# First layer's modulation vectors 2 and 3: four column groups side by side, in eight steps inside the spatial gate's projection

## The chip, the core and the metric

One core of one Trainium2 chip runs the kernel. The metric is the device time of one execution in microseconds (us); the time of a kernel is the median over its runs. The engines are TensorE (PE in the profile, with PEld for its weight loads), VectorE (DVE), ScalarE (ACT), GpSimd (POOL) and SyncE (SP), whose queue issues nearly all the DMAs here.

## The reference, cut to what matters

Two layers of a diffusion backbone on 512 latent and 256 context tokens of width 1024. A layer begins with a modulation: from a conditioning vector it makes six vectors of 1024 (shift, scale and gate of the two sub-layers).

```
def adaln(cvec, w, b, n):
    m = jax.nn.silu(cvec) @ w[:, : n * D_MODEL] + b[: n * D_MODEL]
    return jnp.split(m, n, axis=-1)
...
cmod = adaln(c_ctx, w_mod[l], b_mod[l], 2 if last else 6)
sh1, sc1, g1, sh2, sc2, g2 = [m[:, None, :] for m in adaln(c, w_mod[l], b_mod[l], 6)]
hl = modulate(rms_norm(x_lat, norm1_g[l]), sh1, sc1)
pa, q, k, v, pc = project(hl, P, rope)          # gate A, attention B, convolution C
x_lat = x_lat + g1 * mixer_merge(pa, o, pc, P, lam_init)
h2 = modulate(rms_norm(x_lat, norm2_g[l]), sh2, sc2)
x_lat = x_lat + g2 * conv_ffn(h2, P)
```

Vectors 0 and 1 are needed before the first projection. Vector 2 (gate of the mixing sub-layer) is needed when that sub-layer's output is added, and vector 3 (shift of the channel sub-layer) after that. This case is about vectors 2 and 3 of the first layer, for the latent and the context condition at once: a product of a 2-row matrix with 1024 x 2048 weights.

## The kernel before, in words

**Order of the work.** The program is written as one long list of operations. A scheduler puts each engine's instructions in an order ahead of time: among what is ready in its plan, it takes the earliest in the text, moved by priority offsets (`low(n)` makes a block later, `tc.high_priority` earlier). On the chip every engine goes through its own list in that order; waits are semaphores. All loads named here are issued by SP's queue, in order too.

**The stages around the change.** In layer 0 the projection of the normed tokens (`hhi`, `hlo`, split in two parts for precision) goes over column blocks in the order C (convolution branch), A (spatial gate), K, Q, V. Each block is four chunks of weights (`k2`), each loaded as `raw` (3 buffers, L215), split into `whi` (ACT, L224) and `wlo` (DVE or POOL, L110). Block C is L476 to L488. Blocks A, K, Q and V are in `proj_tok` (L425): for each chunk, six token tiles with four products each (L433, L434), then six tiles with two products each (L441). Each of these 12 tiles is a "step", 48 in all, and a list of hooks may put other work behind a given step.

Block C's result goes through a sigmoid into `cin`, and a depthwise convolution of 31 taps runs on DVE (`cacc`, L691, lowest priority) beside blocks A to Q. Block A's result goes through gelu, a layer norm (L522 to L541, ending in `vbh` and `vbl`) and four small products with the position weights (`pg`, L548), which hooks put behind steps 18 to 25 of block K; transposes (`pt`, L558) follow. The position weights are split into two slots of the `mraw` buffers (L542). The convolution's norm begins with a product `cm` (L653) behind step 41 of block Q.

**Modulation vectors 2 and 3** are made by `mod_rows` (L152), called at L502 to L510 inside `low(RLOW)` with RLOW = 250. The condition, as `cs`, is the stationary operand: 32 columns per slice of 128 inputs, 2 of them used. The weights are the moving operand, 512 columns at a time, so a product uses 32 of the 128 columns of the array. Slice k goes to column group k % 4 (`tile_position=(0, 32 * (k % 4))`), and slices 0 to 3 and 4 to 7 add up in the group's 32 partitions of one PSUM tile `mr`:

```
def part(o, k, w):
    r = 32 * (k % 4)
    T.matmul(o[r:r + 32], cs[:, k], w, start=k < 4, stop=k >= 4, tile_position=(0, r))
...
for k2 in range(KD // 2):
    raw = rp.tile([P, 2, 512], F32, tag=rtag, name="mraw", bufs=rb)
    nc.sync.dma_start(out=raw, in_=w_modH[chunks[0][0] - 2, chunks[0][1] // 4, k2])
    for a in range(2):
        part(acc.rearrange("p c q -> p (c q)"), 2 * k2 + a, raw[:, a])
```

There are four such tiles (2 vectors, 2 halves), so 16 loads of 512 KB into 4 `mraw` buffers and 32 products. Each tile is copied by ACT (`mrow`, L175); then four small products with `sel` (`mt`, L180) add up the four groups and turn the rows into columns, and one DVE addition (L185) puts in the bias.

Vectors 0 and 1 go the same way in pieces of 128 columns (L163 to L167), beside block C.

Of the kernel before, what the change touches and what calls it, by code (L numbers as in the profile page):

```python
# [9 lines left out]
F32 = mybir.dt.float32  # L10
# [6 lines left out]
P = 128  # L17
DM = 1024
KD = DM // P
# [10 lines left out]
COL_A, COL_Q, COL_K, COL_V, COL_C = 0, 512, 1024, 1536, 2048  # L30
# [11 lines left out]
NOSYNC = mybir.DependencyInfo(mybir.DependencyClass.NoSync, mybir.DependencyReason.DATA)  # L42
# [6 lines left out]
MRB, MRW, RAWB, NSQ, NTB, KXB, FTB = 4, 2, 3, 2, 3, 3, 2  # L49

HP, SCP, RSP = 1000, 2, 60
DLOW, RLOW = 150, 250
CLOW = (4000, 1000)

WE = "dpdpdpdddppdpppppddp"
# [25 lines left out]
def tile_backbone(  # L81
# [6 lines left out]
    nc = tc.nc  # L88
    V, S, G, T = nc.vector, nc.scalar, nc.gpsimd, nc.tensor
# [16 lines left out]
    def low(n):  # L106
        return tc.high_priority(offset=-n)
# [44 lines left out]
    def mod_rows(cs, sel, chunks, ps, tag, bufs, rp, rtag, rb):  # L152


        n = len(chunks)
        acc = ps.tile([P, 4, P], F32, tag=tag, name="mr", bufs=bufs)

        def part(o, k, w):
            r = 32 * (k % 4)
            T.matmul(o[r:r + 32], cs[:, k], w, start=k < 4, stop=k >= 4, tile_position=(0, r))  # L160

        if chunks[0][0] < 2:
            for c, (i, f) in enumerate(chunks):  # L163
                raw = rp.tile([P, KD, P], F32, tag=rtag, name="mraw", bufs=rb)
                nc.sync.dma_start(out=raw, in_=w_modN[i, f])
                for k in range(KD):
                    part(acc[:, c], k, raw[:, k])  # L167
        else:
            for k2 in range(KD // 2):
                raw = rp.tile([P, 2, 512], F32, tag=rtag, name="mraw", bufs=rb)  # L170
                nc.sync.dma_start(out=raw, in_=w_modH[chunks[0][0] - 2, chunks[0][1] // 4, k2])
                for a in range(2):
                    part(acc.rearrange("p c q -> p (c q)"), 2 * k2 + a, raw[:, a])
        mrow = rp.tile([P, 4, P], F32, tag="mrow", name="mrow", bufs=MRW)
        S.copy(mrow[:, :n], acc[:, :n])  # L175

        def finish():
            tr = ps.tile([P, 4, 2], F32, tag=tag, name="mt", bufs=bufs)
            for c in range(n):
                T.matmul(tr[:, c], mrow[:, c], sel, start=True, stop=True)  # L180
            for i in sorted({i for i, f in chunks}):
                cl = [c for c in range(n) if chunks[c][0] == i]
                f0, f1 = chunks[cl[0]][1], chunks[cl[-1]][1] + 1
                src = tr[:, cl[0]:cl[-1] + 1:(cl[1] - cl[0] if len(cl) > 1 else 1)]
                V.tensor_add(modv[:, 0, :, i, f0:f1], src.rearrange("p f s -> p s f"),  # L185
                             bmod[:, 0, i, f0:f1].unsqueeze(1).to_broadcast([P, 2, f1 - f0]))

        return finish
# [133 lines left out]
    for l in range(DEPTH):  # L322
        last = l == DEPTH - 1
        NT_KV = NLT + NCT
        NT = NLT if last else NLT + NCT
# [23 lines left out]
        with ExitStack() as ph:  # L349
            sac = ExitStack()  # L350
            sp = pool(sac, f"s1_{l}", side)
            ps = psum_pool(ph, f"ps1_{l}")
# [7 lines left out]
            def wchunk(col, k2, **kw):  # L360
                tags = ("raw", "raw") if k2 % 2 else ("hi", "lo")
                return wsplit_of(("in", col, k2), wsrc(col, k2), [2, 512], wengine(col, k2), tags, **kw)

            if l == 0:
                cs = sp.tile([P, KD, 32], F32, name="cs")
# [109 lines left out]
                    T.matmul(o.rearrange("p a n -> p (a n)"), z[:, :P], z, start=True, stop=False)  # L475
            for k2 in range(KD // 2):  # L476
                wh, wl = wchunk(COL_C, k2, raw=pre.get(k2))
                for a in range(2):
                    k = 2 * k2 + a
                    for s in range(nseg)[::-1]:  # L480
                        t0, t1 = SEG[s]
                        for m in range(4):
                            ms = slice(m * P, (m + 1) * P)
                            o = pc[s][m][:, :t1 - t0]
                            T.matmul(o, wh[:, a, ms], hhi[:, k, t0:t1], start=k == 0 and s == 0, stop=False)
                            T.matmul(o, wh[:, a, ms], hlo[:, k, t0:t1], start=False, stop=False)
                            T.matmul(o, wl[:, a, ms], hhi[:, k, t0:t1], start=False,
                                     stop=k == KD - 1 and (s == 0 or m % 2 == 1))  # L488
# [5 lines left out]
            for s in range(nseg):  # L494
                n = SEG[s][1] - SEG[s][0]
                o0 = PAD if s == 0 else 2 * PAD + LAT
                for c in range(2):
                    sg = sp.tile([P, 512], F32, tag="nsq", name="csg", bufs=2 if l else NSQ)
                    act(sg[:, :n], pc[s][2 + c][:, :n], AF.Sigmoid)
                    V.tensor_mul(cin[:, c, o0:o0 + n], pc[s][c][:, :n], sg[:, :n])  # L500
            if l == 0:
                with low(RLOW):  # L502
                    fin = []
                    for i in (2, 3):
                        for f in (0, 4):
                            fin.append(mod_rows(cs, sel, [(i, f + x) for x in range(4)], ps, "aux", 2, sp, "mraw", MRB))
                            if len(fin) > 1:
                                fin.pop(0)()
                    for f in fin:
                        f()  # L510


            pa = proj_tok(COL_A, range(NT))
            u = sp.tile([P, NT, AW], F32, name="u")
            v = sp.tile([P, NT, AW], F32, name="v")
            mv = sp.tile([P, NT, 2], F32, name="mv")
# [651 lines left out]
```

## Time and profile before

| | |
|---|---|
| median of 3 runs | 1620.43 us (1617.92 to 1620.60) |
| the profiled execution, its own time | 1616.07 us |
| its span, first to last instruction | 1614.0 us |
| mean granted TensorE clock | 0.994 |
| PE busy | 1570.6 us (97%) |
| DVE busy | 1020.4 us (63%) |
| ACT busy | 646.9 us (40%) |
| POOL busy | 105.9 us (7%) |
| chain that ended last | PE 77%, DMA 10%, DVE 6%, ACT 4%, issue 2% |

Read first what share of the span each engine is busy, then, since such a share is a mean over stages with different limits, the same by stage, and in the stage the single instructions in order of time. Times in the rows are microseconds from the start of the span. The times between two instructions' starts on PE tell more than their durations, because products are pipelined.

### The profile page before, as it was taken

How to read it: one execution, taken by the hardware profiler on the slowest of the kernel's cores; microseconds unless marked ns; L12 is line 12 of the kernel's file. 1: busy time of each engine (PE TensorE's matmuls, PEld its weight loads, DVE VectorE, ACT ScalarE, POOL GpSimd, SP SyncE). 2: the span in 40 equal slices, each digit the busy share in tenths (PEclk: the TensorE clock that was granted, in tenths of full speed). 3: DMA queues.
4: the chain of work that ended last, by engine and by line, in shares of the span. 5: the costliest groups of instructions: out<-in, count | busy, mean ns of one | idle time of the engine just before them, and what ended most of it. 6: DMA issues, size and time to landing. Idle time of an engine off the chain costs nothing.

```text
span 1614.0 us, 21207 instructions
## 1 busy us (share of the span) xinstructions
PE 1570.6 (97%) x8186; PEld 1292.4 (80%) x8186; DVE 1020.4 (63%) x1722; ACT 646.9 (40%) x1122; POOL 105.9 (7%) x126
## 2 busy tenths in 40 slices
PE   6999998999999999999999999999999999999999
PEld 4875776778888887878888887887778788888888
DVE  4497878969999983345544244896976544334433
ACT  5431568753532322234433133254764333123321
POOL 1130125310000000000000000000220000000000
PEclk9999999999999999999999999999999999999999
DMA  7625110015255888988611235653022322332232
GB/s 282 212 76 180 56 64 15 14 51 185 85 190 194 285 279 265 289 284 298 207 66 50 60 127 186 205 170 105 27 80 78 104 92 88 95 104 92 92 105 92
DMA packets 83140, 222.93 MB, mean 138 GB/s; under 512 B 12256, under 2 KB 14560, under 8 KB 82912
## 3 DMA queue, kind: packets, MB, share of 16 engines
q1 hardware_dynamic: 83040, 221.59, 41.6%
q8 instruction: 64, 1.05, 0.3%
q14 instruction: 36, 0.29, 0.1%
HBM read 190.10 MB, written 31.46 MB: 137 GB/s over the span
## 4 chain that ended last, share of the span: by engine, by line
PE 77%; DMA 10%; DVE 6%; ACT 4%; issue 2%; SPq 0%; POOL 0%; POOLq 0%; DVEq 0%; ACTq 0%
PE pp L267 10%; PE pp L266 10%; PE pp L268 10%; PE acc L433 5%; PE acc L441 5%; PE acc L434 5%; PE pd L268 4%; PE pd L267 4%; PE pd L266 4%; DMA in<-araw 3%; DMA araw<-in_w_in_dram 3%; PE po L860 3%; PE wo L266 2%; DMA mraw<-in_w_modT_dram 2%; PE wo L267 2%; PE wo L268 2%
## 5 line engine op out<-in xcount | busy, mean ns | idle before, releaser
L268 PE MATMUL pp<-hhi,wlo 128*128 128x512 f32 (+1 forms) x1072 | 380.0, 355 | 4.4 <-DVE wlo L110 4.4
L266 PE MATMUL pp<-hhi,whi 128*128 128x512 f32 (+1 forms) x1072 | 380.6, 356 | 1.7 <-ACT whi L224 1.4
L267 PE MATMUL pp<-hlo,whi 128*128 128x512 f32 (+1 forms) x1072 | 381.4, 356 | 0.8 <-DVE hlo L306 0.8
L224 ACT CAST whi<-raw 128x1024 fp32r<-128x1024 f32 (+1 forms) x167 | 170.9, 1025 | 389.9 <-PE pp L267 203.0
L110 DVE TENSOR_TENSOR wlo<-raw,whi 128x1024 fp32r<-128x1024 f32 (+2 forms) x154 | 185.4, 1206 | 218.4 <-ACT whi L224 211.1
L268 PEld LDWEIGHTS pp<-hhi,wlo 128*128 128x128 f32 x1072 | 202.3, 189 | 36.1 <-DVE wlo L110 5.2
L266 PEld LDWEIGHTS pp<-hhi,whi 128*128 128x128 f32 x1072 | 202.0, 189 | 36.0 <-ACT whi L224 3.3
L267 PEld LDWEIGHTS pp<-hlo,whi 128*128 128x128 f32 x1072 | 202.0, 189 | 32.8 <-DVE hlo L306 1.5
L266 PE MATMUL pd<-gh,whi 128*128 128x512 f32 (+1 forms) x550 | 192.9, 351 | 2.5 <-ACT whi L224 2.5
L268 PE MATMUL pd<-gh,wlo 128*128 128x512 f32 (+1 forms) x550 | 193.6, 352 | 0.8 <-DVE wlo L110 0.8
L267 PE MATMUL pd<-gl,whi 128*128 128x512 f32 (+1 forms) x550 | 193.1, 351 | 0.0
L266 PEld LDWEIGHTS pd<-gh,whi 128*128 128x128 f32 x550 | 103.8, 189 | 18.0 <-ACT whi L224 2.9
L268 PEld LDWEIGHTS pd<-gh,wlo 128*128 128x128 f32 x550 | 104.1, 189 | 15.7 <-DVE wlo L110 1.0
L267 PEld LDWEIGHTS pd<-gl,whi 128*128 128x128 f32 x550 | 103.9, 189 | 15.1
L691 DVE SCALAR_TENSOR_TENSOR cacc<-cin,cw,cacc 128x783 f32<-128x783 f32 (+1 forms) x120 | 103.4, 916 | 3.4 <-ACT cacc L686 3.4
L110 DVE TENSOR_TENSOR araw<-araw,ahi 128x512 f32<-128x512 f32 x56 | 38.5, 691 | 93.3 <-ACT ahi L248 93.2
L1027 DVE TENSOR_TENSOR ft<-ft,pp 128x256 f32<-128x256 f32 (+1 forms) x66 | 39.1, 598 | 74.4 <-PE pp L268 66.7
L196 DVE CUSTOM_DVE_ANT_0 mraw<-mraw,csil,bmod 128x1024 f32<-128x1024 f32 x64 | 81.7, 1279 | 5.9 <-DMA mraw<-in_w_modT_dram 5.5
L248 ACT CAST ahi<-araw 128x512 fp32r<-128x512 f32 x56 | 34.7, 620 | 121.5 <-DMA araw<-in_w_in_dram 83.7
L433 PE MATMUL acc<-whi,hhi 128*128 128x512 f32 x192 | 77.8, 405 | 0.0
L434 PE MATMUL acc<-whi,hlo 128*128 128x512 f32 x192 | 76.9, 401 | 0.0
L101 ACT ACTIVATE ft<-ft 128x768 f32<-128x768 f32 (+1 forms) x44 | 32.6, 740 | 103.2 <-DVE ft L1022 103.2
(224 smaller groups left out, 2599.3 us busy)
## 6 DMA issues: line engine op xcount, KB each, us to landing
raw<-in_w_gv_dram SPq DMA_DIRECT2D x88, 512.0 KB, 3.3
mraw<-in_w_modT_dram SPq DMA_DIRECT2D x64, 512.0 KB, 4.3
raw<-in_w_down_dram SPq DMA_DIRECT2D x34, 512.0 KB, 3.6
wh<-in SPq DMA_DIRECT2D x24, 512.0 KB, 4.4
wl<-in SPq DMA_DIRECT2D x24, 512.0 KB, 4.5
raw<-in_w_in_dram SPq DMA_DIRECT2D x20, 512.0 KB, 4.1
araw<-in_w_in_dram SPq DMA_DIRECT2D x40, 256.0 KB, 3.6
in<-ahi SPq DMA_DIRECT2D x40, 256.0 KB, 4.7
```

What stands on the lines that cost most here:

```text
L110: (eng or V).tensor_sub(o, a, hi.bitcast(F32))
L196: r = V.tensor_tensor_reduce(out=junk, in0=w, in1=csil[:, s], scale=1.0, scalar=bmod[:, l, i, f:f + 1], op0=ALU.mult, op1=ALU.add, accum_o ...
L224: S.copy(hi, raw)
L266: T.matmul(o, lhi, rhi, start=start, stop=False)
L267: T.matmul(o, lhi, rlo, start=False, stop=False)
L268: T.matmul(o, llo, rhi, start=False, stop=stop)
L433: T.matmul(pt[t], hhi[hs], wh[:, a], start=k2 + a == 0, stop=False)
L434: T.matmul(pt[t], hlo[hs], wh[:, a], start=False, stop=False)
L441: T.matmul(pt[t], hhi[hs], wl[:, a], start=False, stop=k2 + 1 == KD // 2 and a == 1)
L691: V.scalar_tensor_tensor(out=cacc[:, c, :cn], in0=cin[:, c, j:j + cn], scalar=cw[:, l, c, j:j + 1], in1=cacc[:, c, :cn], op0=ALU.mult, op1 ...
L860: T.matmul(po, vt[:, kt, hs], at[:, c], start=c == 0, stop=c == nk - 1)
L1027: V.tensor_mul(t[:, a:b], t[:, a:b], pp[s][1][:, :b - a])
```

## The change

The products of vectors 2 and 3 leave `mod_rows` for a generator `mod_groups`, without a lowered priority. It has eight steps, one for four slices k of one half of one vector. A step needs two loaded buffers, issues its four products (k = 3, 2, 1, 0, one in each column group) next to one another, which ordering dependences keep so, issues the two loads of the step after next, and, after every second step, ACT's copy and one step later the four `mt` products. The first four loads are issued at the last chunk of block C; the eight steps stand behind steps 1, 6, 12, 18, 24, 30, 36 and 42 of block A's 48, and the last `mt` products behind step 47. The copy and the `mt` products move to a function of their own (`mod_turn`) unchanged.

```
-DLOW, RLOW = 150, 250
+DLOW = 150
+
+MH = (1, 6, 12, 18, 24, 30, 36, 42, 47)
...
-        if chunks[0][0] < 2:
-            for c, (i, f) in enumerate(chunks):
-                raw = rp.tile([P, KD, P], F32, tag=rtag, name="mraw", bufs=rb)
-                nc.sync.dma_start(out=raw, in_=w_modN[i, f])
-                for k in range(KD):
-                    part(acc[:, c], k, raw[:, k])
-        else:
-            for k2 in range(KD // 2):
-                raw = rp.tile([P, 2, 512], F32, tag=rtag, name="mraw", bufs=rb)
-                nc.sync.dma_start(out=raw, in_=w_modH[chunks[0][0] - 2, chunks[0][1] // 4, k2])
+        for c, (i, f) in enumerate(chunks):
+            raw = rp.tile([P, KD, P], F32, tag=rtag, name="mraw", bufs=rb)
+            nc.sync.dma_start(out=raw, in_=w_modN[i, f])
+            for k in range(KD):
+                part(acc[:, c], k, raw[:, k])
+        return mod_turn(acc, chunks, sel, ps, tag, bufs, rp)
+
+    def mod_groups(cs, sel, ps, tag, bufs, rp, rtag, rb):
...
+        todo = [(i, f, k0) for i in (2, 3) for f in (0, 4) for k0 in (0, 4)]
+        raws = {}
+
+        def load(x):
+            if x < len(todo):
+                i, f, k0 = todo[x]
+                raws[x] = [rp.tile([P, 2, 512], F32, tag=rtag, name="mraw", bufs=rb) for a in range(2)]
                 for a in range(2):
-                    part(acc.rearrange("p c q -> p (c q)"), 2 * k2 + a, raw[:, a])
+                    nc.sync.dma_start(out=raws[x][a], in_=w_modH[i - 2, f // 4, k0 // 2 + a])
+
+        load(0)
+        load(1)
+        yield
+        fin = None
+        for x, (i, f, k0) in enumerate(todo):
+            if k0 == 0:
+                acc = ps.tile([P, 512], F32, tag=tag, name="mr", bufs=bufs)
+            r = raws.pop(x)
+
+            head = None
+            for k in (3, 2, 1, 0):
+                c = slice(32 * k, 32 * k + 32)
+                m = T.matmul(acc[c], cs[:, k0 + k], r[k // 2][:, k % 2], start=k0 == 0, stop=k0 == 4,
+                             tile_position=(0, 32 * k))
+                if head is not None:
+                    tc.add_manual_dep(m.ins, head.name, NOSYNC, reason="next to one another")
+                head = head or m.ins
+            load(x + 2)
+            if fin:
+                fin()
+                fin = None
+            if k0 == 4:
+                fin = mod_turn(acc.rearrange("p (c q) -> p c q", q=P), [(i, f + y) for y in range(4)],
+                               sel, ps, tag, bufs, rp)
+            yield
+        fin()
+        yield
...
             for k2 in range(KD // 2):
                 wh, wl = wchunk(COL_C, k2, raw=pre.get(k2))
+                if l == 0 and k2 == 3:
+                    mg = mod_groups(cs, sel, ps, "aux", 2, sp, "mraw", MRB)
+                    next(mg)
...
-            if l == 0:
-                with low(RLOW):
-                    fin = []
-                    for i in (2, 3):
-                        for f in (0, 4):
-                            fin.append(mod_rows(cs, sel, [(i, f + x) for x in range(4)], ps, "aux", 2, sp, "mraw", MRB))
-                            if len(fin) > 1:
-                                fin.pop(0)()
-                    for f in fin:
-                        f()
...
-            pa = proj_tok(COL_A, range(NT))
+            pa = proj_tok(COL_A, range(NT), [] if l else [(x, lambda: next(mg)) for x in MH])
```

## Rows read from the trace of the kernel before

**Rows 1.** Busy time by stretch: PE, PEld, DVE, ACT, POOL, then clock, DMA share, GB/s.

```profile
60.00:70.00 10.00, 10.00 (x62) 8.92 (x61) 1.23 (x1) 1.05 (x1) 0.00 (x0) 1.00 0.87 299
...
72.40:107.10 34.70, 34.70 (x148) 27.32 (x148) 31.37 (x33) 11.09 (x18) 12.85 (x2) 1.00 0.22 72
107.10:165.80 58.70, 58.70 (x256) 34.12 (x255) 46.68 (x63) 17.00 (x30) 6.24 (x2) 1.00 0.48 159
165.80:205.50 39.70, 39.04 (x195) 31.19 (x194) 32.62 (x74) 23.84 (x48) 5.43 (x2) 1.00 0.18 54
```

**Rows 2.** Waits of PE between 158 and 245 us: total, times, longest.

```profile
PE pk L621 <- DVE ks L110: 0.7, 1, 0.7
```

**Rows 3.** One line of the code, L160: its products and their forms.

```profile
L160 PE MATMUL mr<-mraw,cs x320: 272/273/617, 12.3 to 151.1; 128*32 128x128 f32 x128, 128*32 128x512 f32 x32
```

**Rows 4.** Timeline of PE, 72 to 151 us: start, duration, what, count of records.

```profile
72.08 0.40 PE L487 MATMUL accC<-hhi,wlo 128*128 128x512 f32 x1
72.41 1.04 PE L160 MATMUL mr<-mraw,cs 128*32 128x512 f32 x2
73.38 0.51 PE L433 MATMUL acc<-whi,hhi 128*128 128x512 f32 x1
73.72 0.40 PE L434 MATMUL acc<-whi,hlo 128*128 128x512 f32 x1
...
117.46 1.06 PE L160 MATMUL mr<-mraw,cs 128*32 128x512 f32 x6
118.45 0.49 PE L441 MATMUL acc<-wlo,hhi 128*128 128x512 f32 x1
...
123.08 1.05 PE L160 MATMUL mr<-mraw,cs 128*32 128x512 f32 x4
124.06 0.50 PE L434 MATMUL acc<-whi,hlo 128*128 128x512 f32 x1
...
126.73 0.28 PE L180 MATMUL mt<-sel,mrow 128*128 128x2 f32 x2
...
127.18 0.28 PE L180 MATMUL mt<-sel,mrow 128*128 128x2 f32 x2
...
150.67 1.05 PE L160 MATMUL mr<-mraw,cs 128*32 128x512 f32 x4
```

**Rows 5.** Chain that ended last, in order of time: start, us, what, records.

```profile
34.80 0.79 PE mt L180 x8
35.58 0.57 PE mr L160 x16
...
104.45 2.80 PE acc L441 x12
```

**Rows 6.** Timeline of SP's queue: start, time to the last issue's end, what.

```profile
83.67 26.77 SPq L216 DMA_DIRECT2D raw<-in_w_in_dram  x4
115.73 26.45 SPq L171 DMA_DIRECT2D mraw<-in_w_modH_dram  x12
```

**Rows 7.** DMA issues: count, KB each, us to landing.

```profile
mraw<-in_w_modH_dram SPq DMA_DIRECT2D x16, 512.0 KB, 3.8
```

**Rows 8.** Timelines of POOL and DVE, 90 to 203 us, and of PE.

```profile
90.59 10.44 POOL L110 TENSOR_TENSOR wlo<-raw,whi 128x1024 fp32r<-128x1024 f32 x1 [14.44 <-issue]
...
130.37 1.75 DVE L110 TENSOR_TENSOR vbl<-v,vbh 128x1536 fp32r<-128x1536 f32 x1
...
195.02 0.69 DVE L650 TENSOR_TENSOR cin<-cacc 128x512 f32<-128x512 f32 x1
...
202.67 1.02 PE L653 MATMUL cm<-cin,ones 128*128 128x512 f32 x2
```

**Rows 9.** Timelines: the gate's first product in layer 0, then layer 1 with its `vbl`.

```profile
152.83 0.42 PE L266 MATMUL pg<-vbh,wmraw 128*128 128x384 f32 x1
...
1044.67 1.22 DVE L110 TENSOR_TENSOR vbl<-v,vbh 128x1024 fp32r<-128x1024 f32 x1
...
1047.69 0.28 PE L266 MATMUL pg<-vbh,whi 128*128 128x256 f32 x1
```

More of the change, by code (lines that the diff above doesn't have):

```diff
@@ L174, in mod_rows, with mod_turn @@
+    def mod_turn(acc, chunks, sel, ps, tag, bufs, rp):
+        n = len(chunks)
         mrow = rp.tile([P, 4, P], F32, tag="mrow", name="mrow", bufs=MRW)
```

## The prediction

> **What bounds the kernel now.** I read the busy time by stretch first. In blocks A and K, from 72.4 to 165.8 us, PE is busy the whole time (34.70 of 34.70 and 58.70 of 58.70 us) at a granted clock of 1.00, the upper of its two levels (2.4 GHz), and in block Q nearly so, 39.04 of 39.70 [rows 1]. DVE is busy 31.37 of 34.70 us in block A but only 46.68 of 58.70 in block K. DMA is nearly empty in block A (72 GB/s) and half full in block K (159), while the ten microseconds before reached 299 GB/s. So TensorE sets the time here, and each microsecond taken off its list is won unless another engine then holds it up. The list of PE's waits says how near that is: between 158 and 245 us there is one wait, 0.7 us for `ks` of DVE [rows 2]. Then I went through PE's timeline to see what the modulation products cost among the others.
>
> A plain product of 512 columns costs 0.233 us: 12 of them take 2.80 [rows 5]. The 32 modulation products of vectors 2 and 3 have two records each (in all 320 records for 160 products of both kinds [rows 3]). They don't stand where the text has them, ahead of block A: one does, the other 31 lie in block K, up to 150.67 us [rows 4]. What the reader is to see is the count of records against the time. A single product (2 records) at 72.41 lets the next instruction start at 73.38, 0.97 later; two of them (4 records) at 123.08 take 0.98, and three (6 records) at 117.46 take 0.99 [rows 4]. Products in different column groups run at the same time, so a visit costs the same whatever it holds. The 64 records lie in 18 visits: five of one product, one of three, twelve of two.
>
> **The change, part by part.** *The visits removed.* A visit costs more than its 0.97. The last product of block C starts at 72.08 and the second product of block A at 73.72; with two plain products between these starts it would be 0.467, so the visit costs 1.64 - 0.47 = 1.17 us, 0.1 on either side of it included [rows 4]. 18 x 1.17 = 21.1 us leave PE's list.
>
> *The visits added.* There are eight, with four products each. No row has four of 512 columns. From below, a visit can cost no less than one of a single product, 1.17; from above, four in sequence would be 4 x 0.97 + 0.2 = 4.08. The nearest rows are the three side by side, 0.99, and the pieces of 128 columns beside block C, where eight products (16 records, two rounds of four) take 0.57 [rows 5], 0.29 a round, though a quarter of 0.97 for each of the eight would be 1.9. Four groups do run at once. From one to three products a visit grew by 0.02, so I take 1.19. 8 x 1.19 = 9.5 us. The difference is 21.1 - 9.5 = 11.6 us less on PE.
>
> The Trainium skill (TensorE: Matmul & The Clock Gate, section Measured speedup vs the span model) speaks against so much: three column tiles of 512 columns gained 2.38 there, four row tiles 3.07, not 3 and 4. By that, as an estimate, a visit of four would be 0.2 + 0.97 x 4 / 3.07 = 1.46 us, the eight 2.2 us dearer, and the time 1611.4. The trace does not agree for three: 0.99 stands here, where a gain of 2.38 would make it 1.22.
>
> *The `mt` products.* The 16 stay. Most stand alone among plain ones: from 126.73 to 127.18 there are one of them and one plain product, 0.45, so one costs 0.22 [rows 4], 3.5 in all. Now four stand together; such a set took 0.79 beside block C [rows 5], four sets 3.2. That saves 0.3.
>
> *The loads.* The 16 loads move on SP's queue, the first four ahead of the loads of constants and of block A's weights, the other 12 from 115.73 to 142.18 [rows 6] into block A. Block A gets 12 x 0.52 = 6.3 MB on top of the 2.5 MB that it moves now, in 34 + 9.5 + 3 = 46 us: 190 GB/s, against 299 seen [rows 1]. A step's loads go out right after the step before last, 8.7 us or more ahead of use (eleven steps, 32 products, and one visit), and such a load lands in 3.8 [rows 7]; two of them in a row 5.6 at 299 GB/s. I cost the data at nothing. Its cover is this lead of some 3 us; what is gone with it stands in the rivals. The four first loads cost nothing either: the constants they hold back are first read when block C is through, and block A's first weights can't be split before block C frees its buffers.
>
> *ACT, DVE, POOL.* The four copies of `mrow` and four additions of `modv` are the same instructions as before, only earlier. DVE in block A is full of convolution taps of the lowest priority, which give way; POOL gets nothing new.
>
> *What is late next.* Block A ends 11 us later, block K is 23 us shorter, so everything from block Q on comes earlier. Two things could then be late. First `vbl`, which the gate's products need: now it is ready at 132.12, 24.9 us after block A's last product (107.25) [rows 5, 8], and nobody waits, since the gate's first product stands at 152.83 [rows 9]; its weights are split into buffers that the modulation products hold until late. In the text it stands behind step 18, 60 products or 14.0 us into block K. So the wait is between 0 and 10.9 us. Layer 1, with the same code and no modulation products, is the nearest row: there the gate's first product comes 1.8 us after `vbl` (1045.89 to 1047.69) [rows 9], and PE waits for nothing. I take 0 and keep 10.9 for the range. Second, DVE: it idles 12.0 us in block K now, and loses about that much time. Taps left over can go into block Q, where DVE has 7 us to spare (39.70 - 32.62) and `cin` is ready 7.0 us before `cm` is multiplied (195.71 to 202.67) [rows 8]. The wait for `ks`, 0.7, sits on this chain [rows 2]; it could vanish, or grow by what doesn't fit, 12.0 - 7.0 = 5.0. I let it double: +0.7.
>
> The sum: -11.6 - 0.3 + 0.7 = **-11.2 us**. Against the profiled execution, 1616.07 (its span of 1614.0 and 2.1 around it), that is 1604.9. The median of the runs is 4.4 above that execution, 0.27%, and so the forecast for the median is 1620.4 - 11.2 = **1609.2 us**.
>
> **The rivals.**
>
> *The gate waits a little* (chance 0.14). The scheduler puts `pg` where its plan has `vbl` ready, and on the chip `vbl` comes 2 to 8 us later than planned. For it: in layer 0 POOL and DVE disturb each other, one split of POOL took 10.44 us [rows 8], and layer 1 has no such split. Against it: the 1.8 us to spare in layer 1. Time: 1609.2 + 5 = 1614, 1611 to 1617.
>
> *The data are late* (0.08). SP's queue is in order, and the four weight loads from 83.67 on are spread over 26.77 us because each waits for a buffer [rows 6]. The one that waits for that POOL split would be free at about 105 in the new order (101.03 and three visits more). If the seventh step's loads stand behind it, they land some 6 us later, at 111, while the step is due at 72.3 + 25.2 + 6 x 1.19 + 2 x 0.79 = 106.2. PE waits 5 us: 1614.
>
> *The convolution or the gate eats it all* (0.05). Products kept at step 18 with `vbl` as late as now: a wait of 10.9, time 1620.
>
> *Slower* (0.05). The same place, one step further: the taps that DVE can no longer do in block K's idle time stand ahead of the norm of the gate in its list, so that `vbl` comes later than 24.9 us after block A. It decides from a chain of 14.0 + 11.2 = 25.2 us on, if `pg` stands at step 18. With half of the 12.0 us of idle time filled, the chain is 30.9, the wait 16.9, the time 1609.2 + 16.9 = 1626. For it: DVE is nearly full in block A. Against: the taps have the lowest priority, and `pg` has been moved off step 18 before.
>
> *It doesn't do what it says* (0.02): the four go in sequence after all, 8 x 4.08 = 32.6 us in place of 21.1, 1631. The 0.57 of [rows 5] and the 0.99 of [rows 4] speak against it.
>
> **How the numbers follow.** The forecast has 0.66. A measurement of this kernel tells 0.2%, 3.2 us, from no change, so faster means below 1617.2: forecast, a little wait and late data, 0.88. Same is the case of 1620, 0.05; slower the last two, 0.07. The range takes in, below, both waits of 1.4 us gone, three switches of 0.1 saved where `mt` stands right behind `mr`, and 1 us for the spread of the runs: 1606.5. Above, it takes in the skill's visit, late data and most of the little wait: 1616.5. What is left out is 0.15.
>
> **What would show it.** In the changed kernel's trace, PE should have eight visits of 8 records between 73 and 115 us, each some 0.99 us from its first start to the next product, and none in block K. Block A should end near 119 us, block K near 155, block Q start 11 us earlier than now. `pg` should stand around 20 to 24 us into block K with no wait of PE. PE's list of waits up to 245 us should stay under 2 us. A wait of PE on `mraw` would show late data, one on `vbl` at `pg` the gate, one on `cin` at `cm` the convolution; visits of over 1.2 us would show that four don't fit side by side. The forecast is wrong if block Q starts less than 8 us earlier, or if it starts so much earlier and the gain is lost behind it.

## The result, and the profile after

The changed kernel took 1609.35 us in the median of six runs (1607.56 to 1615.05); the kernel before, on the same chips, 1618.54 in the median of six (1617.92 to 1620.60). The ratio is 0.9947 with an interval of 0.9929 to 0.9965, so a gain of 5.7 to 11.5 us. The forecast was 1609.2, a gain of 11.2. That the two times lie so close is partly luck: the six runs of before have a median 1.9 lower than the first three, on which the forecast was built, so that the gain between the medians is 9.2. Execution against execution the gain is smaller: 1616.07 before, 1607.56 after, 8.5 us.

| | before | after |
|---|---|---|
| span of the profiled execution | 1614.0 | 1605.4 |
| mean granted clock | 0.994 | 0.994 |
| PE busy | 1570.6 | 1560.6 |
| DVE, ACT, POOL busy | 1020.4, 646.9, 105.9 | 1019.8, 647.0, 100.5 |
| length of block K, first product to first product of Q | 60.38 | 39.67 |

PE has 10.0 us less work, but the span fell by only 8.6. Where the rest went is seen in blocks A and K. The timeline of PE, after, from the end of block C to block Q (it answers to [rows 4]; `mr` is line 196 now, the block's products 473, 474 and 481, `mt` 220, `pg` 306 and 307):

```profile
72.39 1.04 PE L196 MATMUL mr<-mraw,cs 128*32 128x512 f32 x2
73.36 0.50 PE L473 MATMUL acc<-whi,hhi 128*128 128x512 f32 x1
...
74.50 1.06 PE L196 MATMUL mr<-mraw,cs 128*32 128x512 f32 x6
75.49 0.51 PE L473 MATMUL acc<-whi,hhi 128*128 128x512 f32 x1
...
80.35 1.07 PE L196 MATMUL mr<-mraw,cs 128*32 128x512 f32 x8
81.34 3.06 PE L481 MATMUL acc<-wlo,hhi 128*128 128x512 f32 x12
84.33 1.06 PE L196 MATMUL mr<-mraw,cs 128*32 128x512 f32 x8
85.33 1.05 PE L220 MATMUL mt<-sel,mrow 128*128 128x2 f32 x8
86.24 0.48 PE L473 MATMUL acc<-whi,hhi 128*128 128x512 f32 x1
...
115.36 1.06 PE L196 MATMUL mr<-mraw,cs 128*32 128x512 f32 x8
...
120.15 0.40 PE L473 MATMUL acc<-whi,hhi 128*128 128x512 f32 x1
...
139.25 0.62 PE L306 MATMUL pg<-vbh,wmraw 128*128 128x384 f32 x2 [2.15 <-ACT vbh L572]
...
143.34 0.45 PE L307 MATMUL pg<-vbl,wmraw 128*128 128x384 f32 x1
...
159.82 0.40 PE L473 MATMUL acc<-whi,hhi 128*128 128x512 f32 x1
```

Read the starts. Eight records, that is four products, let the next instruction start 0.99 to 1.00 us later (80.35 to 81.34, 84.33 to 85.33). The first step stands in two pieces, one product at 72.39 and three at 74.50, so there are nine visits, not eight. Block K starts at 120.15 and has none left. And at 139.25 PE waits for `vbh`, which it did not before. Busy time by stretch, blocks A and K, after (columns as in [rows 1]):

```profile
72.29:120.15 47.86, 47.86 (x242) 31.51 (x241) 40.03 (x50) 15.54 (x27) 5.38 (x2) 1.00 0.50 182
120.15:159.82 39.67, 37.52 (x169) 30.18 (x168) 39.54 (x50) 14.35 (x24) 8.69 (x2) 1.00 0.21 63
```

In block A PE is busy throughout. In block K DVE is now the full engine, 39.54 of 39.67 us, where it had 12 us of idle time [rows 1], and PE is not: it lacks 2.15, the wait at `pg`.

To follow the gain, this table gives the start of some stages in each run (first product of block K, of block Q, of the convolution's norm `cm`, of the attention `pq`, of the last large stage of the layer `pp`), and the span:

| kernel | K | Q | K's length | `cm` | `pq` | `pp` | span |
|---|---|---|---|---|---|---|---|
| before | 107.09 | 167.47 | 60.38 | 202.7 | 244.2 | 404.2 | 1614.0 |
| changed | 120.15 | 159.82 | 39.67 | 194.6 | 236.1 | 395.6 | 1605.4 |
| e1, gate later | 119.87 | 159.41 | 39.54 | 194.3 | 235.9 | 396.4 | 1606.2 |
| e2, first step joined | 119.22 | 158.88 | 39.66 | 193.7 | 235.2 | 395.3 | 1607.0 |
| e7, e1 and e2 | 119.29 | 158.83 | 39.54 | 193.8 | 235.3 | 395.1 | 1604.0 |
| e5, groups at the old place | 106.61 | 160.18 | 53.57 | 195.4 | 236.9 | 397.0 | 1607.0 |
| e3, one group | 139.94 | 181.12 | 41.18 | 216.3 | 257.9 | 415.9 | 1627.0 |
| e4, pairs | 128.88 | 169.87 | 40.99 | 204.6 | 246.1 | 406.2 | 1619.0 |
| e6, no POOL in block K | 119.73 | 156.75 | 37.02 | 191.9 | 233.4 | 393.4 | 1603.6 |
| e8, e2 and e6 | 119.17 | 156.33 | 37.16 | 191.5 | 233.0 | 393.0 | 1606.6 |
| e9, e6's edit in before | 107.06 | 167.44 | 60.38 | 202.6 | 244.1 | 404.2 | 1615.0 |
| r1, the change again | 119.59 | 159.26 | 39.67 | 194.0 | 235.6 | 395.0 | 1612.7 |

Block Q starts 7.65 us earlier (forecast: 11.9 less on PE's list), the attention 8.1, the span ends 8.6 earlier. So the loss against the forecast is made before block Q. The wait for `ks` of [rows 2], which I let double, is gone from PE's list.

### The profile page after: what moved, and what is told of

It reads as the page before. It is cut to its first block, busy times and chain, and to the rows that moved or that the text cites. A ratio compares the mean times of both kernels' runs of the same rounds, so it can differ in the third digit from the quotient of the medians.

```text
span 1605.4 us, 21200 instructions
## 1 busy us (share of the span) xinstructions
PE 1560.6 (97%) x8186; PEld 1291.3 (80%) x8186; DVE 1019.8 (64%) x1722; ACT 647.0 (40%) x1122; POOL 100.5 (6%) x126
## 4 chain that ended last, share of the span: by engine, by line
PE 51%; DMA 6%; DVE 1%; ACT 1%; issue 0%; POOLq 0%; SPq 0%; DVEq 0%; ACTq 0%
PE pp L307 8%; PE pp L308 8%; PE pp L306 8%; PE pd L308 5%; PE pd L307 4%; PE pd L306 4%; DMA in<-araw 3%; DMA araw<-in_w_in_dram 2%; PE acc L473 2%; PE acc L481 2%; PE acc L474 2%; PE po L892 1%; PE wo L306 1%; PE wo L307 1%; PE wo L308 1%; PE pss L844 1%
## 5 line engine op out<-in xcount | busy, mean ns | idle before, releaser
L308 PE MATMUL pd<-gh,wlo 128*128 128x512 f32 (+1 forms) x550 | 193.8, 352 | 0.8 <-DVE wlo L112 0.8
```

Source lines behind the costliest of these rows:

```text
L308: T.matmul(o, llo, rhi, start=False, stop=stop)
```

## The experiments

The theory after the result: four products side by side do cost what one costs; what is missing went into a split first step (1.2 us) and into a wait of the gate's products for DVE (2 to 3 us). The rivals: the gain is from the new place and not from the grouping; or `pg` was only put too early in PE's list.

**Four in one group, e3.** All four products of a step go to column group 0, one behind another, and the accumulation runs over all eight slices. The sum is the same.

```diff
-                c = slice(32 * k, 32 * k + 32)
-                m = T.matmul(acc[c], cs[:, k0 + k], r[k // 2][:, k % 2], start=k0 == 0, stop=k0 == 4,
-                             tile_position=(0, 32 * k))
+                c = slice(0, 32)
+                m = T.matmul(acc[c], cs[:, k0 + k], r[k // 2][:, k % 2],
+                             start=k0 == 0 and k == 3, stop=k0 == 4 and k == 0, tile_position=(0, 0))
```

`mt` then reads 32 partitions in place of 128.

> The changed kernel with all products of vectors 2 and 3 in column group 0 (the eight slices add up there, and the turning products read 32 rows in place of 128); the same steps, loads and neighbours. Theory (side by side means at the same time, only in different column groups): a step's four products go in sequence, 32 x 0.97 + 9 x 0.2 = 32.8 us in place of 9 x 1.18 = 10.6, so block K starts 22 us later, at 142, and the span is 1627. Rival (standing next to one another in few visits is what saves, the group does not matter): span 1605 to 1607.

It took 1628.80 us in one execution beside 1617.24 of before. The timeline of PE, the step that stands at 80.35 in the changed kernel:

```profile
81.73 3.62 PE L196 MATMUL mr<-mraw,cs 128*32 128x512 f32 x8
85.28 3.07 PE L481 MATMUL acc<-wlo,hhi 128*128 128x512 f32 x12
```

The same eight records take 3.55 us, against 0.99 in four groups. Block K starts 19.8 later than in the changed kernel (22 expected, with 0.97 a product) and the span is 21.6 longer. The grouping is what pays, and the kernel is slower than before without it.

**Pairs, e4.** Two products in a step, 16 steps in the same stretch, each with one load.

```diff
-MH = (1, 6, 12, 18, 24, 30, 36, 42, 47)
+MH = (1, 3, 6, 9, 12, 15, 18, 21, 24, 27, 30, 33, 36, 39, 42, 45, 47)
...
-            for k in (3, 2, 1, 0):
...
+            for k in (1, 0):
+                g = 32 * (k0 % 4 + k)
+                m = T.matmul(acc[g:g + 32], cs[:, k0 + k], r[:, k], start=k0 < 4, stop=k0 >= 4, tile_position=(0, g))
```

> The changed kernel with two products to a step and 16 steps in block A (17 visits, since the first is split as in the changed kernel); the same products, groups and block, and the same order of PE's list behind block A. Theory (a visit costs 1.18 us whatever it holds): 8 visits more, block K starts 9.4 us later at 129.6, PE's wait at pg stays near 2.2, and the span is 1614.8, about that of the kernel before. Rival (place and priority bring the gain, not the visits): span 1605 to 1608.

1620.75 us in one execution. Timeline of PE:

```profile
80.95 1.05 PE L195 MATMUL mr<-mraw,cs 128*32 128x512 f32 x4
81.93 1.66 PE L479 MATMUL acc<-wlo,hhi 128*128 128x512 f32 x6
83.52 1.05 PE L195 MATMUL mr<-mraw,cs 128*32 128x512 f32 x4
```

Two products take 0.98. The first step is split here too, so there are 17 visits, eight more than in the changed kernel. Block K starts 8.73 later, though block A begins 0.55 earlier (71.84 against 72.39): 9.3 us for eight visits, 1.16 each. The attention starts 10.0 later, 1.9 later than before, and the span is 1619.0 where 1614.8 was expected. Moving the products into block A without grouping them by four wins nothing: what counts is the number of visits.

A part of the miss stands in block K, which is 1.3 us longer than in the changed kernel (40.99 against 39.67):

```profile
147.99 1.01 PE L304 MATMUL pg<-vbh,wmraw 128*128 128x384 f32 x2 [2.15 <-ACT vbh L570]
148.79 0.63 PE L471 MATMUL acc<-whi,hhi 128*128 128x512 f32 x1
149.21 0.63 PE L472 MATMUL acc<-whi,hlo 128*128 128x512 f32 x1
```

The wait at `pg` is the same 2.15 as in the changed kernel, but behind it plain products stand 0.42 to 0.43 apart in place of 0.23, until 151.35: from 149 to 151 us the granted clock is 0.50, the lower of its two levels (1.2 GHz). In e3 it falls to 0.50 as well (158 to 160 us), behind a wait of 2.19, and block K is 1.5 longer. In the changed kernel, in e2 and in r1 it stays at 1.00 behind the same wait. What decides it, these runs don't show. Without it, as an estimate, e4 would start the attention some 0.6 later than before and not 1.9.

**Groups of four at the old place, e5.** The kernel before, with its low priority, and only the four products of a half tied to one another:

```diff
-            for k2 in range(KD // 2):
-                raw = rp.tile([P, 2, 512], F32, tag=rtag, name="mraw", bufs=rb)
-                nc.sync.dma_start(out=raw, in_=w_modH[chunks[0][0] - 2, chunks[0][1] // 4, k2])
-                for a in range(2):
-                    part(acc.rearrange("p c q -> p (c q)"), 2 * k2 + a, raw[:, a])
+            for k0 in (0, 4):
+                r = [rp.tile([P, 2, 512], F32, tag=rtag, name="mraw", bufs=rb) for a in range(2)]
+                for a in range(2):
+                    nc.sync.dma_start(out=r[a], in_=w_modH[chunks[0][0] - 2, chunks[0][1] // 4, k0 // 2 + a])
+                head = None
+                for k in (3, 2, 1, 0):
+                    m = part(acc.rearrange("p c q -> p (c q)"), k0 + k, r[k // 2][:, k % 2])
+                    if head is not None:
+                        tc.add_manual_dep(m.ins, head.name, NOSYNC, reason="next to one another")
+                    head = head or m.ins
```

> The kernel before, with its low priority and its place, but each half vector's loads and products taken four slices at a time, the four products tied together as in the change. Its list has 12 visits (six for the first eight products, then six of four) in place of 18, all but one in block K, and the gate's products late as before. Theory (visits are what costs): six visits of 1.17 us less, span 1607.0, and no wait at pg. Rival (the move into block A, away from block K, is what brings the gain): span 1612 to 1614.

1609.72 us in the median of four, ratio 0.9953 (0.9938 to 0.9969). The products stand in 12 visits in place of 18; two of them in PE's timeline:

```profile
123.52 1.07 PE L160 MATMUL mr<-mraw,cs 128*32 128x512 f32 x8
...
143.33 1.06 PE L160 MATMUL mr<-mraw,cs 128*32 128x512 f32 x8
```

Six visits fewer are worth 6 x 1.17 = 7.0 us. Block K is 6.8 shorter (53.57 against 60.38), 1.14 a visit; block Q starts 7.3 earlier, of which 0.5 is there before block A begins (71.94 against 72.41). The span is 7.0 shorter. PE's list of waits, 72 to 245 us, has nothing for `pg`: its products stand behind the modulation as before. So grouping alone gives nearly the whole measured gain. The changed kernel saves three visits more (3.5 us) and gives most of that back at `pg`.

**Gate later, e1.** The gate's products are hooked behind steps 30 to 37 of block K.

Here the text ahead of the prediction is wrong, and the prediction with it. Both have `pg` behind step 18 of block K, the former behind steps 18 to 25. The table of hooks has one entry per layer, and layer 0 has the first, (4, 1): steps 4 to 11. Step 18 is layer 1's. The scheduler moves the products anyway: in the changed kernel the first `pg` stands behind 72 products of block K.

```diff
-AH = ((4, 1), (18, 1))
+AH = ((30, 1), (18, 1))
```

> The changed kernel with the gate's products hooked behind steps 30 to 37 of block K in layer 0, in place of 4 to 11; nothing else. Theory (in the changed kernel they stand too early in PE's list, and PE stands still until vbh and vbl come): PE's wait of 2.15 us at the first pg and some 0.5 us of broken runs around the others go, block Q starts at about 157.1 in place of 159.8, and the span is 1602.9 in place of 1605.4. Rival (DVE is behind and the wait only moves): block Q starts at 157.1 too, but PE then waits 2 us or more for ks at the first pk or for cin at cm, and the span stays at 1605.

1608.24 us in the median of four, ratio 0.9942 (0.9924 to 0.9960); block K 39.54 against 39.67. PE's waits, 72 to 245 us:

```profile
PE pss L844 <- ACT e L103: 2.2, 3, 0.9
PE pg L306 <- DVE yA L581: 1.3, 1, 1.3
PE pg L307 <- DVE vbl L112: 0.5, 1, 0.5
PE pk L653 <- DVE ks L112: 0.4, 1, 0.4
```

The wait did not go away, it moved: `pg` at 142.27 no longer waits for `vbh`, but for `vbl`, then for `yA`, which frees the PSUM tile, then `pk` for `ks`. All three are DVE's. (The `pss` line belongs to the attention.) That `pg` was merely listed too early, which was the theory (span 1602.9), is refuted: DVE is behind. The rival had this, and the span (1605 expected, 1606.2 measured), but looked for the wait at `ks` or `cin`, where most of it stands inside block K.

**No POOL in block K, e6.** Why it is behind is seen in the timeline of DVE, POOL and ACT in block K of the changed kernel:

```profile
120.45 2.39 POOL L112 TENSOR_TENSOR wlo<-raw,whi 128x1024 fp32r<-128x1024 f32 x1 [21.24 <-DVE st L558]
120.67 3.00 DVE L723 SCALAR_TENSOR_TENSOR cacc<-cin,cw,cacc 128x783 f32<-128x783 f32 x1
124.40 1.00 DVE L723 SCALAR_TENSOR_TENSOR cacc<-cin,cw,cacc 128x783 f32<-128x783 f32 x1
...
126.41 4.81 DVE L723 SCALAR_TENSOR_TENSOR cacc<-cin,cw,cacc 128x783 f32<-128x783 f32 x5
128.85 6.30 POOL L112 TENSOR_TENSOR wlo<-raw,whi 128x1024 fp32r<-128x1024 f32 x1 [6.01 <-PE acc L481]
131.13 1.75 DVE L570 TENSOR_TENSOR v<-v,lnv 128x1536 f32<-128x1536 f32 x1
132.80 3.17 DVE L723 SCALAR_TENSOR_TENSOR cacc<-cin,cw,cacc 128x783 f32<-128x783 f32 x1
135.90 1.75 DVE L571 TENSOR_TENSOR v<-v,lnv 128x1536 f32<-128x1536 f32 x1
137.73 1.47 ACT L572 CAST vbh<-v 128x1536 fp32r<-128x1536 f32 x1 [2.29 <-DVE v L571]
```

A tap takes 1.00 alone. The two that run beside a split of POOL take 3.00 and 3.17. The second stands between the multiplication and the addition of the gate's norm (L570, L571), so `vbh` comes some 2.2 us later than it would, as long as PE's wait at `pg`. The experiment gives POOL's two splits of block K to DVE, 1.22 us each:

```diff
-WE = "dpdpdpdddppdpppppddp"
+WE = "dpdpdpddddddpppppddp"
```

> The changed kernel with block K's second and third weight chunks split on DVE in place of POOL. In the changed kernel two convolution taps that run beside a POOL split take 3.0 and 3.2 us in place of 1.0, both inside the chain from block A's end to vbh (19.1 us). Theory (POOL and DVE disturb each other, and this makes vbh late): the chain is 16 to 17 us, PE's wait at pg falls under 0.5 us, span 1603. Rival (the order of DVE's list makes it late, and a split on DVE only adds to it): the chain is 19 us or more, the wait 2 us or more, span 1605 to 1607.

1605.69 us in one execution. Timeline of DVE, ACT and PE:

```profile
122.01 1.01 DVE L723 SCALAR_TENSOR_TENSOR cacc<-cin,cw,cacc 128x783 f32<-128x783 f32 x1
...
128.74 1.22 DVE L112 TENSOR_TENSOR wlo<-raw,whi 128x1024 fp32r<-128x1024 f32 x1
...
132.49 1.03 DVE L723 SCALAR_TENSOR_TENSOR cacc<-cin,cw,cacc 128x783 f32<-128x783 f32 x1
135.28 1.48 ACT L572 CAST vbh<-v 128x1536 fp32r<-128x1536 f32 x1 [0.29 <-DVE v L571]
137.47 0.51 PE L306 MATMUL pg<-vbh,wmraw 128*128 128x384 f32 x2
```

DVE has two more splits to do and is done earlier: every tap takes 1.0, and `vbh` ends 17.0 us after block A (119.73 to 136.76) in place of 19.05. `pg` stands at 137.47 without a wait, and block K is 37.02 long, 2.65 less. That is the size of the wait's damage, and its cause. The attention starts 2.7 earlier than in the changed kernel, but 0.4 of this is there before block K begins (119.73 against 120.15), and a wait of 0.6 for `ks` takes back a part of the 2.65.

Only the second slow tap counts. L570 starts 10.98 us into block K in the changed kernel and 11.09 here (130.82), although the first tap takes 1.01: by then DVE has also done the two splits. From L570 to L571 it is 4.77 there and 2.61 here (133.43), and this is the whole gain. The plan also puts `pg` four products later here, behind 76 of block K; behind 72, 16.8 us, it would have waited some 0.2 for `vbh`.

A full DVE is not needed for the wait. In e3 most taps are done before block K, and DVE is busy for only 25.10 of its 41.18 us; `pg` waits 2.19 all the same, with a tap of 3.10 and a pair of `cin` operations of 3.24 beside POOL's two splits.

**The same edit in the kernel before, e9.** One thing could still be said: that this edit is simply better everywhere.

```diff
-WE = "dpdpdpdddppdpppppddp"
+WE = "dpdpdpddddddpppppddp"
```

> The kernel before with block K's second and third chunks split on DVE, as a control. Theory (POOL and DVE disturb each other there too, but the gate's products stand so late that nobody waits): vbh and vbl come 2 us or more earlier after block A than the 21.0 and 25.0 us of the kernel before, and the time stays as it was, ratio 0.998 to 1.002. Rival (fewer POOL splits are a gain by themselves): 2 to 3 us less here too, ratio 0.998 or below.

1616.97 us in the median of ten, ratio 1.0000 (0.9989 to 1.0011); block K 60.38 in both. The time is as the theory has it, but the chain is not: 2 us or more were expected, and from block A to the end of `vbh` it is 0.6 shorter (21.0 to 20.4), to the end of `vbl` not at all (25.0 in both). The slow tap between the norm's two operations is gone here too (3.15 before, 1.03 now), but DVE first does the split that POOL did:

```profile
120.36 1.22 DVE L110 TENSOR_TENSOR wlo<-raw,whi 128x1024 fp32r<-128x1024 f32 x1 [1.48 <-PE acc L441]
```

It has to wait 1.48 us for PE to free its buffer, and the norm behind it starts 1.5 later. Nobody notices any of this, since `pg` stands 45.7 us into block K in that kernel (107.09 to 152.83 [rows 9], 152.80 with the edit). The disturbance between POOL and DVE is there before the change too, but only with `pg` as early as the change puts it does it cost something. As a control e9 is weak, since it hardly shortens the chain.

**First step joined, e2.** The first of the four products (k = 3) was ready while nothing else was, right behind block C, and the three tied to it came only after the next tile's four products. Here it is ordered behind block A's first tile:

```diff
-            head = None
+            head = None if x else seen[-1]
             for k in (3, 2, 1, 0):
...
-                head = head or m.ins
+                if k == 3:
+                    head = m.ins
...
-                            T.matmul(pt[t], hlo[hs], wh[:, a], start=False, stop=False)
+                            seen.append(T.matmul(pt[t], hlo[hs], wh[:, a], start=False, stop=False).ins)
```

> The changed kernel with the first product of the first step held behind block A's first tile, so that the first step's four products stand together: 8 visits in place of 9. Theory (a visit costs 1.18 us whatever it holds): block K starts at 119.0 in place of 120.15, the gate's chain starts that much earlier too, PE's wait at pg stays at 2.15, and the span is 1604.2. Rival (taps stand ahead of the chain in DVE's list, so that vbh comes at a fixed time): the wait grows to 3.3 us and the span stays at 1605.4.

1609.12 us in one execution. Timeline of PE:

```profile
73.24 0.40 PE L476 MATMUL acc<-whi,hlo 128*128 128x512 f32 x1
73.56 1.06 PE L196 MATMUL mr<-mraw,cs 128*32 128x512 f32 x8
74.56 0.50 PE L475 MATMUL acc<-whi,hhi 128*128 128x512 f32 x1
```

The step is whole, block K starts 0.93 earlier, the attention 0.9. PE's wait at `pg` is 2.1 as before, so the rival (`vbh` at a fixed time) falls. The span of that execution does not show the gain (1607.0 against 1605.4, 1604.2 expected); what lies behind the attention spreads by more than that, as the last run shows.

**Both together: e7 (e1 and e2) and e8 (e2 and e6).** The edits are those above.

> Both edits together: the first step's four products in one visit, and the gate's products behind steps 30 to 37. Theory: the two gains add up, 1.2 + 2.5 us, span 1601.7, ratio to the kernel before 0.992 where the change alone has 0.9947. Rival (what is won ahead of block Q is given back to DVE there): span 1604 to 1605, ratio 0.994 to 0.995.

> The changed kernel with both edits that won time by themselves: the first step's four products in one visit, and block K's second and third chunks split on DVE. Theory (independent losses of 1.0 and 2.7 us at the start of the attention): block K starts at about 119 and is 37.0 us long without a wait at pg, the first pq of the attention stands at 232.4 where the changed kernel has 236.1, ratio to the kernel before 0.992 to 0.993. Rival (later stages give it back): the first pq is 3 us earlier, and the span is 1605 all the same.

e7: 1607.05 us in the median of five, ratio 0.9936 (0.9924 to 0.9949). Its attention starts at 235.3, no earlier than with e2 alone (235.2), and the span is the rival's 1604.0: as in e1, DVE takes back what the later `pg` gives. e8: 1607.26 in the median of six, ratio 0.9939 (0.9916 to 0.9962), its runs from 1598.53 to 1613.07. PE's waits of e8, 72 to 245 us:

```profile
PE pss L846 <- ACT e L103: 2.4, 3, 0.9
PE pss L846 <- POOL qh L829: 1.1, 1, 1.1
PE pk L655 <- DVE ks L112: 0.6, 1, 0.6
```

No wait for `pg`, and the attention starts at 233.0, 11.2 us earlier than before: the whole forecast gain, at that point. But the span of that execution is 1606.6, the rival's "later stages give it back", and in the median time the gain shows only in part. Neither version can be told from the changed kernel by its interval. Their medians are some 2 us below the changed kernel's 1609.35 (e8's 3.9 below r1's on the same chip), which is not certain.

**The change once more, r1,** unaltered, beside e8 and e9 on their chip.

> The changed kernel once more, on the same chip as the two others, for their differences. Both theories: ratio to the kernel before 0.994 to 0.996, block K 39.7 us long with one wait of 2.1 us at pg. Rival (the wait belongs to one execution): another length or no wait.

1611.16 us in the median of ten (1606.55 to 1614.82), ratio 0.9962 (0.9948 to 0.9976). Here the gain is 5.9 us between the medians, where the first measurement has 9.2; the two intervals overlap, and a gain of 11.2 (a ratio of 0.993) lies at the edge of the first and outside the second. Block K is 39.67 long with one wait of 2.1 at `pg`, as in the first measurement, so the wait does not belong to one execution. The profiled execution reaches `pp` as early as that of the first measurement (395.0 against 395.6), and then loses 7.9 us: 3.6 up to layer 1 (its first copy of `kx` stands at 984.49 against 981.51), 4.3 in it. PE's waits between 400 and 985 us, first the changed kernel's first profile:

```profile
PE pp L308 <- DVE wlo L112: 4.1, 3, 2.5
PE pd L306 <- ACT whi L264: 2.0, 1, 2.0
PE pp L306 <- ACT whi L264: 1.2, 2, 0.8
PE pd L308 <- DVE wlo L112: 0.8, 1, 0.8
```

then r1:

```profile
PE pp L308 <- DVE wlo L112: 5.1, 5, 2.2
PE pd L306 <- ACT whi L264: 3.9, 2, 3.6
PE pd L308 <- DVE wlo L112: 1.2, 2, 0.8
```

These are waits for split weights, 8.1 us in all against 10.2. In layer 1 a stretch shows more. Busy time by stretch, the first profile of the changed kernel:

```profile
1200.00:1220.00 20.00, 18.32 (x93) 14.93 (x92) 7.62 (x13) 4.99 (x11) 0.00 (x0) 1.00 0.48 168
```

and r1:

```profile
1200.00:1220.00 20.00, 15.82 (x63) 11.99 (x62) 5.31 (x9) 4.66 (x9) 0.00 (x0) 0.91 0.48 159
```

PE waits there for weight loads (`wh` and `wl`, 4.2 us between 1120 and 1250, against 1.7 in the first profile). Behind the longest of these waits, 2.2 us up to 1208.63, it is granted 0.69 and 0.74 from 1209 to 1215, its lower level for a part of the time, in place of 1.00. So one kernel's executions differ by up to 8 us, in places that the change doesn't touch. Why the weights come later in one execution than in another was not settled.

## Why the prediction was right, and where not

The direction and the main mechanism, fewer visits, were right; the median was right partly by luck. The size was 2.6 us off for the profiled execution (-8.6 of span, forecast -11.2), and 2.0 and 5.3 for the medians of the two measurements. By the steps of the sum:

**The visits.** *Removed, 18 x 1.17 = 21.1*: as forecast, none is left in block K, and e5 and e4 give the price of a visit anew (6.8 us of block K for six fewer, 9.3 at its start for eight more). *Added, 8 x 1.19 = 9.5*: the price was right, 0.99 to 1.00 us to the next product for four. The estimate from 3.07, the gain of four row tiles in the Trainium skill (TensorE: Matmul & The Clock Gate, section Measured speedup vs the span model), 1.46 a visit with its switches, is not borne out: four in four column groups took 0.99, 1.19 with the switches, where the same four in one took 3.55 (e3), a gain of 3.6. The upper bound of four in sequence, 4.08 with its switches, was 0.3 above e3's 3.55 + 0.2. The count was wrong: nine visits, because the ordering holds a step's products behind its first, but holds nothing before the first. Worth 1.2 us in the sum and 0.93 when undone (e2).

**The `mt` products, 0.3 saved.** Nothing was saved: three of the sets stand behind a visit and take 0.91 each (85.33 to 86.24), the fourth stands among plain products and takes 0.80 (118.80 to 119.60); together 3.5, the old price. The 0.79 of a set beside block C [rows 5], which I took for all, fits only the fourth.

**The loads, nothing.** Right. PE never waits for `mraw`; they land in 4.1 us, and block A moves 182 GB/s, forecast 190. The rival of late data falls.

**The gate's wait, 0, with 10.9 kept for the range.** This is the step that failed, and the largest one: 2.15 us of wait and some 0.5 of smaller ones behind it, 2.65 together by e6. The row of layer 1 that I called nearest had 1.8 us to spare, but has no POOL split in that stretch; I wrote so myself under the rival and gave it 0.14. What I put at nothing was a convolution tap between the norm's two operations that stands still for one such split, 3.17 us in place of 1.00 (e6). The bound itself was worked out from the wrong step (18 for 4). From step 4, 16 products or 3.7 us into block K, it would have been 24.9 - 3.7 = 21.2 and not 10.9. It would have made the rival of 1620 some 10 us dearer. It would not have changed the forecast, since the scheduler places `pg` later than its hook in both kernels, nor the range, which ends at 1616.5 and so never held the 10.9 that I said I kept for it. Nor was `vbl` what is waited for: the first products need only `vbh`.

**DVE, `ks` doubled, +0.7.** Wrong in sign: the wait of 0.7 vanished. DVE did become full in block K (39.54 of 39.67), as the two idle totals suggested, but nothing waits longer for `ks`. Where `pg` no longer waits for `vbh` (e1, e6), `ks` waits again, 0.4 and 0.6; this is no strict exchange, since e3 has both waits, 2.2 and 0.7.

The sum, mended: -11.9 + 1.2 for the ninth visit + 0.3 for `mt` + 2.7 for the gate makes -7.7; measured at block Q -7.65. With the wait of 0.7 gone it should be -8.4 at the attention, and is -8.1.

**The signs that were named.** Block A ended at 120.15 (near 119 expected), `pg` stood 19.1 us into block K (20 to 24), block Q came 7.65 earlier, under the 8 that I had named as the point where the forecast is wrong. By that mark of its own it failed for block Q, while the time stayed inside the range.

Of the rivals, "the gate waits a little" is what happened, at 2.7 instead of 5. The slower one (taps ahead of the gate's norm, 16.9 us of wait) had the right place: a tap does stand between the norm's multiplication and its addition. But it is one tap that costs 2.2, by POOL, and not several by their number. The time of the last rival, 1631, comes to 1632 by its own terms.

## What to carry to other kernels

Count what a small-column product costs as a visit, not as a product: four in four column groups cost here what one does (0.99 against 0.97), so group them first, and then see where they stand (e5 wins as much by grouping alone). When work is taken out of a stretch on the bounding engine, what hid behind it is uncovered: list each chain that ends in that stretch with its lead, and look for instructions in it whose duration depends on another engine. A dependence that ties products to the first of them does not keep the first from leaving early; tie it to what precedes as well.

## What the runs showed of the hardware

**POOL and DVE take turns.** In block K of the changed kernel POOL's split runs from 120.45 to 122.84; the tap that starts at 120.67 ends at 123.67, 0.83 after POOL. POOL's second split is issued at 128.85, while DVE goes from one two-input operation to the next; it ends at 135.15, 2.35 after 132.80, where DVE's multiplication is through, and the tap that starts there ends 0.82 after POOL again. So neither slows the other down, one stands still until the other is through: 2.39 of work takes 6.30 on POOL, 1.0 takes 3.17 on DVE. The Trainium skill (SBUF — State Buffer, section Who interferes with whom) says so: a DVE instruction with two inputs in SBUF contends with a GpSimd instruction that reads SBUF, and the loser stands still rather than sharing. The trace agrees to within 0.2 us of the plain durations. In the 10.44 of [rows 8] I had seen that the two disturb each other, but had priced POOL's side alone; the other half is that DVE pays as well.

**Products in one column group** behind one another cost less than single ones: four take 3.55, so the three behind the first 0.86 each, where a single one among plain products takes 0.97.

**A wait of 2.2 us can bring TensorE's clock down, or not.** Behind waits of 2.15 and 2.19 us at `pg` the granted clock fell to 0.50 in e4 and e3, for some 3 us, and block K took 1.3 and 1.5 us more. Behind the same wait in the changed kernel, e2 and r1 it stayed at 1.00. So such a wait cost 2.2 us in some executions and 3.5 in others.

**Executions of one kernel** with the same start differ by up to 8 us behind the attention (r1). Later weights and a lower clock behind one wait for them (0.69 and 0.74) are seen there; they were not added up to the 8 us. A change worth 2 us early in the kernel, as e2 or e6, is read from where the attention starts, not from the time.
